# First block tile of a conv-gated MLP on one Trainium2 core: the plain tile's end and the down weights behind the copy of its first chain, down units between its last chains, three squares by transfers

## The chip, the cores and the metric

The kernel runs on one core of one Trainium2 chip. The metric is device time in microseconds (us). The time before is 1180.66 us, the median of three runs (1180.66 to 1180.72). The engines are TensorE (PE, with its weight loads as PEld), VectorE (DVE), ScalarE (ACT), GpSimd (POOL) and SyncE (SP), which issues loads. Each works off its own instructions in order and waits on semaphores for the others.

## The reference: what is computed

The reference is a trunk of two layers over 512 tokens of width 1024, in float32. Each layer has a mixer (an mLSTM or a band attention, with memory cross-attention) and then the part that matters here, a gated MLP with a causal convolution of width 3 and 2816 hidden columns:

```python
def conv_ffn(h, w_up, conv_w, conv_b, w_down):
    u, g = jnp.split(h @ w_up, 2, axis=-1)
    g = causal_dwconv(g, conv_w, conv_b)
    return (jax.nn.silu(g) * u) @ w_down

x = x + conv_ffn(rmsnorm(x, norm_ffn_g[l]), ffn_w_up[l], ffn_conv_w[l], ffn_conv_b[l], ffn_w_down[l])
```

The RMS norm divides each token by the root of the mean square over its 1024 features. The kernel keeps activations transposed: eight tiles `xT[0..7]` of 128 features by 512 tokens, so the mean square is a sum over the eight tiles and over the partitions.

## The kernel before

**Precision.** Each float32 operand is split into a high part (a cast on ACT, line 144) and a low part (a subtraction on DVE, line 145). A product is three matmuls (lines 198 to 200): high by high, high by low, low by high.

**The norm.** `OutProjection.finish` (line 720) ends the mixer of a layer. For each tile j it adds the projection to `xT[j]` on DVE (line 725), stores the tile by a transfer on POOL's queue (line 726, pinned in order), hands it to `norm.add` and scales it into a high and a low part (lines 341 and 342). `Norm.add` squares the tile on ACT. Tile 0's square starts the sum; those of tiles 1 to 4 (`j < SENT`, with `SENT = 5`) are added to it by accumulating transfers on POOL's queue (line 296), each of which waits for the one before; tile 5's square starts a second sum (`new`); tiles 6 and 7 are added to that on DVE (line 298). After tile 7 `norm.join()` (line 301) adds the first sum to the second on DVE. `Norm.finish` splits the sum, adds it over the partitions with matmuls by ones (line 311), and forms the row of inverse roots.

**The MLP.** The 2816 hidden columns are 22 tiles. Tiles 0 and 1 are plain: a gate chain and an up chain of 24 full-width matmuls each (`plain_chain`), then `plain_gate` (line 778): gate by norm row (L780), last tap on ACT (L763), two taps on DVE (L756), SiLU on ACT (L784); then `plain_end` (line 787): the multiplication with the up part on DVE (L788), and `keep`, which splits the result into the high and low part of `hid`.

Tiles 2 to 21 are block tiles: the gate and up products of a tile are computed together by a scheme with seven half-size products instead of eight, on sums and differences of weight blocks and of activations. The activations' sums are made in `block_sums` (lines 797 and 806), the weights' ones in `Forms` (L995). A step (line 915) has seven chains of 12 half-width matmuls: a11, a12, s2, s1, s3, a22, s4. Four of them (a11, s2, s3, a22) use the same PSUM buffer r1, and between two of them ACT copies the result out (line 933 for a11, line 923 for the others). s1 and s4 share r3; DVE reads it (line 946) before s4 may start. DVE adds the a12 chain at line 936. In the same step the next tile's weights are prepared (`nxt`) and the previous tile's taps, SiLU and gating are done (`tail`).

**Down units.** The product with `w_down` is cut into units of a few hidden tiles by 128 output columns. Units of the step are computed into two PSUM buffers (tag `tr`), copied by ACT (line 832) and added in memory by a transfer of POOL's queue (line 836). Tile 2's step has four units (hidden tiles 0 and 1), the steps behind it mostly two. Their weights are loaded on SP's queue (line 157), and split by `split_down` into the buffer pair `wh2`, `wl2`, of which there is one.

**The order.** Inside `later` the order of PE, ACT and DVE is the one written out by hand (`manual_schedule`, line 903). Outside it, in `finish`, `first_plain` and `second_plain`, a planner places instructions by its own cost model. Before the change `plain_end` of tile 1 and `split_down` stand in `second_plain` (lines 893 and 896), so the planner places them; in the step of tile 2 all four units stand behind the last chain, and those of later tiles behind s3.

Of the kernel before, what the change touches and what calls it, by code (L numbers as in the profile page):

```python
# [18 lines left out]
S = 512  # L19
KT = D // P  # L20
# [9 lines left out]
FT = DFF // P  # L30
# [12 lines left out]
PLAIN, LAST, LATE = 2, 6, 8  # L43
# [4 lines left out]
LATE_ROW = {11: 2, 12: 3, 13: 4, 14: 5, 15: 0, 16: 1, 17: 6, 18: 7}  # L48
UNITS = {PLAIN + i: tuple((i, j) for j in range(*LOADS[i][2:])) for i in range(len(LOADS))}

H, SENT = S // 2, 5


def f(ap):
# [4 lines left out]
def trunk(  # L59
# [34 lines left out]
    def sb(tag, shape, dtype=F32):  # L94
        count[0] += 1
        return pool.tile(shape, dtype, tag=tag, name=f"{tag}{count[0]}", bufs=bufs[tag])

    def ps(tag):
        count[0] += 1
        return psum.tile([P, S], F32, tag=tag, name=f"p{tag}{count[0]}", bufs=pbufs[tag])  # L100
# [101 lines left out]
    def project(w, c0, act, tag="mm", parts=None):  # L202


        n = len(act)
        wh, wl = parts or weights(rows(w, c0, P), n, P)
        o = ps(tag)
        for k in range(n):
            mm3(o, wh[:, k, :], wl[:, k, :], act[k][0], act[k][1], k == 0, k == n - 1)
            yield  # L210
        return o

    def run(gen):
        while True:
            try:
                next(gen)
            except StopIteration as end:
                return end.value
# [57 lines left out]
    def logarithms():  # L276

        pin(A.preload_act_table_set("natural_log_exp_and_others"))

    class Norm:  # L280
# [22 lines left out]
        def finish(self):  # L303


            parts = [sb("t", [P, S], F32R) for _ in range(2)]
            split(*parts, self.acc)
            yield 7.4
            o = ps("sc")
            for i, part in enumerate(parts):  # L310
                nc.tensor.matmul(o, onesr, part, start=i == 0, stop=i == 1)
            v, r, t = sb("rb", [P, S]), sb("t", [P, S]), sb("t", [P, S])
            A.activation(t, o, AF.Ln, scale=1.0 / D, bias=eps)
            V.tensor_scalar(v, o, 1.0 / D, EPS, op0=ALU.mult, op1=ALU.add)
            A.activation(r, t, AF.Exp, scale=-0.5)
            A.activation(t, r, AF.Square)
            yield 4
            V.scalar_tensor_tensor(t, t, -0.5, v, op0=ALU.mult, op1=ALU.mult)
            self.row = sb("rb", [P, S])
            V.scalar_tensor_tensor(self.row, t, 1.5, r, op0=ALU.add, op1=ALU.mult)  # L320
# [18 lines left out]
    def scaled(t, g):  # L339
        hi, lo = sb("u", [P, S], F32R), sb("u", [P, S], F32R)  # L340
        A.activation(hi, t, AF.Copy, scale=g)
        V.scalar_tensor_tensor(lo, t, g, f(hi), op0=ALU.mult, op1=ALU.subtract)  # L342
        return hi, lo
# [86 lines left out]
    norm = Norm()  # L430
# [44 lines left out]
    with tc.manual_schedule(engines={mybir.EngineType.PE, mybir.EngineType.Activation, mybir.EngineType.DVE}):  # L475

        logarithms()
        w = ps("mm")
# [17 lines left out]
        def step(products, os_, k, order):  # L496
            for a, b in order:
                for i, o in enumerate(os_):
                    c = slice(i * P, (i + 1) * P)
                    st, mv = kv[k][a], memT[k][b]  # L500
                    first, last = (k, (a, b)) == (0, order[0]), (k, (a, b)) == (KT - 1, order[-1])
                    if products == "keys":
                        nc.tensor.matmul(o, st[:, c], mv, start=first, stop=last)
                    else:
                        nc.tensor.matmul(o, mv[:, c], st[:, MEM:], start=first, stop=last)
# [194 lines left out]
    class OutProjection:  # L700
# [19 lines left out]
        def finish(self, mixer):  # L720
            logarithms()
            norm = mixer.norm
            for j in range(KT):
                o = self.o[j] if j in self.o else run(project(self.w, j * P, self.mixes))
                V.tensor_add(xT[j], xT[j], o)
                pin(G.dma_start(xspill[j], xT[j]))
                norm.add(xT[j], sent=j < SENT, new=j == SENT)
                mixer.act.append(scaled(xT[j], mixer.gain[:, j : j + 1]))
                if j == KT - 1:
                    norm.join()  # L730
                for _ in range(EARLY[mixer.l].get(j, 0)):
                    next(mixer.forms)

    class ChannelMixer:
# [148 lines left out]
        def second_plain(self):  # L883
            og = run(self.plain_chain(1, False, self.next_gate))
            ou = run(self.plain_chain(1, True))
            prep = Forms(self, PLAIN)
            prep.split_up()
            prep.sums()
            prep.split_second()
            acc = self.plain_gate(1, og)  # L890
            prep.sum_third()
            prep.split_sums()
            self.plain_end(acc, ou)
            prep.sum_fourth()
            prep.split_gate()
            prep.split_down()
            return prep

        def later(self, prep):


            tail = None
            with tc.manual_schedule(
                engines={mybir.EngineType.PE, mybir.EngineType.Activation, mybir.EngineType.DVE}
            ):
                for j in range(PLAIN, FT):
                    self.beside()
                    tail, prep = self.step(j, prep, Forms(self, j + 1) if j + 1 < FT else None, tail)
            for part in (
                tail.last_block, tail.scaled, tail.first_tap, tail.scaled_up,  # L910
                tail.second_tap, tail.third_tap, tail.silu, tail.gated, tail.split,
            ):
                part()

        def step(self, j, w, nxt, tail):
            def then(o, *names):
                for name in names if o is not None else ():
                    getattr(o, name)()

            def sum_products(o, r, w, i):  # L920

                self.products(r, w, self.t(i))
                A.copy(o, r[:, :H])  # L923

            new = Tail(self, j)
            late = self.load_late(LATE_ROW[j]) if j in LATE_ROW else None
            then(tail, "last_block", "scaled")
            w.split_fourth()
            then(tail, "scaled_up")
            r1, r2, new.r3 = ps("mm"), ps("mm"), ps("sc")  # L930
            new.up, new.u3, new.pre = sb("t", [P, S]), sb("t", [P, S]), sb("t", [P, S])
            self.products(r1, w.a11, self.b(0, 0), True)
            A.copy(new.up[:, :H], r1[:, :H])  # L933
            then(tail, "first_tap", "second_tap", "third_tap")
            self.products(r2, w.a12, self.b(1, 0), True)
            V.tensor_tensor(out=new.up[:, :H], in0=new.up[:, :H], in1=r2[:, :H], op=ALU.add)
            sum_products(new.up[:, H:], r1, w.s2, 2)
            then(tail, "silu")
            then(nxt, "sums")
            self.products(new.r3, w.s1, self.t(1), True)  # L940
            then(tail, "gated")
            then(nxt, "split_second", "sum_third")
            sum_products(new.u3[:, :H], r1, w.s3, 3)
            then(tail, "split")
            then(nxt, "split_up")
            V.tensor_tensor(out=new.pre[:, H:], in0=new.u3[:, :H], in1=new.r3[:, :H], op=ALU.add)
            if j > PLAIN:
                w.down_products(0, 2)
            then(nxt, "split_sums", "sum_fourth")
            if j > PLAIN:  # L950
                w.add_down(0)
            then(nxt, "split_gate")
            if j > PLAIN:
                w.add_down(1)
                then(nxt, "split_down")
            sum_products(new.pre[:, :H], r1, w.a22, 4)
            if j > PLAIN:
                w.down_products(2, 4)
            self.products(new.r3, w.s4, self.b(1, 1))
            if j == PLAIN:  # L960
                w.down_products(0, 2)
                w.add_down(0)
                w.add_down(1)
                w.down_products(2, 4)
                then(nxt, "split_down")
            w.add_down(2)
            w.add_down(3)
            if late is not None:
                self.late_row(LATE_ROW[j], late)
            return new, nxt  # L970
# [102 lines left out]
    def channel_mixer(mixer):  # L1073
        mixer.first_plain()
        mixer.buffers()
        prep = mixer.second_plain()
        run(mixer.forms)
        mixer.later(prep)
        reload_x()
        return mixer.hid[FT - LAST :]  # L1080

# [295 lines left out]
    mixer = ChannelMixer(0, col["gffn"][:, 0:8], more_rows)  # L1377
# [14 lines left out]
    norm = norm2  # L1392
# [123 lines left out]
    mixer = ChannelMixer(1, col["gffn"][:, 8:16], lambda: None)  # L1516
# [125 lines left out]
```

## Time and profile before

| What | Value |
|---|---|
| Median of three runs | 1180.66 us |
| The profiled execution's own time | 1179.68 us |
| Its span | 1178.0 us |
| PE busy | 1161.6 us |
| DVE busy | 987.0 us |
| ACT busy | 747.1 us |
| Step of tile 2, layer 0 | 296.00 to 314.38 us |
| Step of tile 2, layer 1 | 851.46 to 869.97 us |

How to read it: the profile is one execution, with times in us from the span's start. In a timeline a row has start, duration, engine, line, operation, output and input, the count of merged instructions, and in brackets the idle time before it with what ended it. In the waits a row has the waiting engine and line, what it waited for, and the total, the count and the longest. Matmuls are pipelined, and their ends are modelled, so a PE that is shown as busy may still lose time between two starts.

### The profile page before, as it was taken

The numbers are of one execution on the slowest core, as the hardware profiler recorded it, in microseconds if no ns is written. First come the engines' busy times: TensorE is split into PE (matmuls) and PEld (weight loads), VectorE is DVE, ScalarE is ACT, GpSimd is POOL, SyncE is SP. The second block draws the span as 40 slices with busy tenths as digits, with TensorE's granted clock in tenths as the row PEclk, the third lists the DMA queues.
The fourth block names the chain that finished last, engine by engine and source line by source line (L and its number), as shares of the span: only waits on it lengthen the run. The fifth ranks groups of instructions, "written<-read, shape, count | busy, mean of one in ns | idle before, by whom it ended". The sixth has DMA issues, their size and how long they took to land.

```text
span 1178.0 us, 19355 instructions
## 1 busy us (share of the span) xinstructions
PE 1161.6 (99%) x7221; PEld 1035.6 (88%) x7221; DVE 987.0 (84%) x1766; ACT 747.1 (63%) x1345; POOL 158.2 (13%) x262
## 2 busy tenths in 40 slices
PE   9999999999999999999999999999999999999997
PEld 9988888887899999999888888778789999999986
DVE  6776788889799988888788888897979998888865
ACT  6448677656666655555676576777666765555545
POOL 1111101011121222111020000101010111111100
PEclk9999999999999999999999999999999999999999
DMA  8645315256368877776573323236535667777651
GB/s 294 217 109 148 77 55 152 78 148 184 111 159 189 201 191 193 177 176 133 159 222 94 90 67 100 88 106 177 154 116 152 154 148 177 178 179 171 134 162 72
DMA packets 205904, 173.37 MB, mean 147 GB/s; under 512 B 9352, under 2 KB 178030, under 8 KB 205810
## 3 DMA queue, kind: packets, MB, share of 16 engines
q1 hardware_dynamic: 184914, 123.93, 35.7%
q0 software_dynamic: 20320, 47.15, 20.0%
q8 instruction: 57, 0.93, 0.3%
q10 hardware_dynamic: 576, 1.05, 0.2%
q14 instruction: 37, 0.30, 0.1%
HBM read 133.09 MB, written 40.85 MB: 148 GB/s over the span
## 4 chain that ended last, share of the span: by engine, by line
PE 87%; DVE 4%; issue 4%; ACT 3%; DMA 2%; POOL 0%; POOLq 0%; DVEq 0%; ACTq 0%
PE pmm L198 16%; PE pmm L199 16%; PE pmm L200 16%; PE ptr L199 5%; PE ptr L198 5%; PE ptr L200 5%; PE psc L198 4%; PE psc L200 4%; PE psc L199 4%; PE psc L612 2%; PE ptr L1464 1%; DMA rb<-t 1%; DVE wl L145 1%; PE ptr L1485 1%; PE ptr L1486 1%
## 5 line engine op out<-in xcount | busy, mean ns | idle before, releaser
L198 PE MATMUL pmm<-u,wh 128*128 128x256 f32 (+1 forms) x992 | 334.7, 338 | 0.2 <-ACT u L144 0.2
L199 PE MATMUL pmm<-u,wh 128*128 128x256 f32 (+1 forms) x992 | 331.9, 335 | 0.5 <-DVE u L342 0.5
L200 PE MATMUL pmm<-u,wl 128*128 128x256 f32 (+1 forms) x992 | 332.3, 335 | 0.0
L145 DVE TENSOR_TENSOR wl<-wr,wh 128x1024 fp32r<-128x1024 f32 (+4 forms) x172 | 193.4, 1125 | 77.1 <-ACT wh L144 76.5
L144 ACT CAST wh<-wr 128x1024 fp32r<-128x1024 f32 (+4 forms) x172 | 167.0, 972 | 77.4 <-PE pmm L199 33.7
L200 PEld LDWEIGHTS pmm<-u,wl 128*128 128x128 f32 x992 | 186.3, 188 | 18.8
L199 PEld LDWEIGHTS pmm<-u,wh 128*128 128x128 f32 x992 | 186.6, 188 | 17.2 <-DVE u L342 0.9
L198 PEld LDWEIGHTS pmm<-u,wh 128*128 128x128 f32 x992 | 186.4, 188 | 16.6 <-ACT u L144 1.0
L198 PE MATMUL ptr<-u,wh 128*128 128x512 f32 x272 | 106.5, 392 | 0.0
L199 PE MATMUL ptr<-u,wh 128*128 128x512 f32 x272 | 106.3, 391 | 0.0
L200 PE MATMUL ptr<-u,wl 128*128 128x512 f32 x272 | 105.8, 389 | 0.0
L144 ACT CAST fh<-pt 128x512 fp32r<-128x512 f32 x120 | 74.8, 624 | 38.2 <-DVE pt L995 35.3
L198 PE MATMUL pmm<-u,fh 128*128 128x256 f32 x320 | 89.2, 279 | 3.1 <-ACT t L933 2.1
L923 ACT COPY t<-pmm 128x256 f32<-128x256 f32 x120 | 45.0, 375 | 69.3 <-PE pmm L200 69.2
L199 PE MATMUL pmm<-u,fh 128*128 128x256 f32 x320 | 88.6, 277 | 0.0
L200 PE MATMUL pmm<-u,fl 128*128 128x256 f32 x320 | 88.4, 276 | 0.0
L145 DVE TENSOR_TENSOR fl<-pt,fh 128x512 fp32r<-128x512 f32 x120 | 82.4, 687 | 3.9 <-ACT fh L144 0.7
L756 DVE SCALAR_TENSOR_TENSOR t<-t,cols,t 128x511 f32<-128x511 f32 x88 | 65.9, 749 | 8.1 <-ACT t L763 6.7
L198 PEld LDWEIGHTS pmm<-u,fh 128*128 128x128 f32 x320 | 60.1, 188 | 6.0 <-ACT t L933 2.5
L198 PE MATMUL psc<-u,wh 128*128 128x256 f32 (+1 forms) x208 | 63.2, 304 | 0.0
L200 PE MATMUL psc<-u,wl 128*128 128x256 f32 (+1 forms) x208 | 62.9, 303 | 0.0
L199 PE MATMUL psc<-u,wh 128*128 128x256 f32 (+1 forms) x208 | 62.9, 302 | 0.0
(358 smaller groups left out, 2629.0 us busy)
## 6 DMA issues: line engine op xcount, KB each, us to landing
wr<-in_ffn_w_up_dram SPq DMA_DIRECT2D x48, 512.0 KB, 8.5
pt<-in_ffn_w_up_dram SPq DMA_DIRECT2D x40, 512.0 KB, 7.6
wr<-in_ffn_w_down_dram SPq DMA_DIRECT2D x32, 512.0 KB, 5.2
wr<-in_a_w_in_dram SPq DMA_DIRECT2D x20, 512.0 KB, 3.7
xspill<-bias POOLq DMA_DIRECT2D x32, 256.0 KB, 6.9
without_row<-bias POOLq DMA_DIRECT2D x24, 256.0 KB, 4.3
wr<-in_w_kv_dram SPq DMA_DIRECT2D x12, 512.0 KB, 3.9
without_row<-t POOLq DMA_DIRECT2D x24, 256.0 KB, 4.1
```

Of the source, the lines that this page charges most:

```text
L144: high = A.copy(hi, src) if on_act else V.tensor_copy(hi, src)
L145: low = V.tensor_tensor(out=lo, in0=src, in1=f(hi), op=ALU.subtract)
L198: nc.tensor.matmul(o, lh, rh, start=first, stop=False, skip_group_check=more)
L199: nc.tensor.matmul(o, lh, rl, start=False, stop=False, skip_group_check=more)
L200: nc.tensor.matmul(o, ll, rh, start=False, stop=last, skip_group_check=more)
L612: nc.tensor.matmul(o, a, b, start=first and i == 0, stop=i == 1)
L756: V.scalar_tensor_tensor(acc[:, n:], src[:, : S - n], self.fw[:, c * FT + j : c * FT + j + 1], acc[:, n:], op0=ALU.mult, op1=ALU.add,)
L923: A.copy(o, r[:, :H])
L1464: nc.tensor.transpose(tp[:, b * P : (b + 1) * P], es[T, h][:, b * P : (b + 1) * P], ident)
L1485: nc.tensor.matmul(o2[:, s * P :], w, hi_at(pts[h], s, s, TT - s), start=s == 0, stop=False)
L1486: nc.tensor.matmul(o2[:, s * P :], w, lo_at(pts[h], s, s, TT - s), start=False, stop=s == TT - 1)
```

## The change

Three edits in one:

1. `plain_end` of tile 1 and `split_down` of tile 2 leave `second_plain` and stand in the hand-written step of tile 2, behind ACT's copy of the a11 chain.
2. The four units of tile 2 stand as in the other steps: two behind s3, two behind a22. The next tile's `split_down` stands ahead of the copy of a22.
3. `SENT` is 4 instead of 5: the squares of tiles 1 to 3 are added by transfers, tile 4's starts the second sum, tiles 5 to 7 are added on DVE. `join` stands ahead of tile 7's `norm.add`.

```diff
-H, SENT = S // 2, 5
+H, SENT = S // 2, 4
...
                 pin(G.dma_start(xspill[j], xT[j]))
+                if j == KT - 1:
+                    norm.join()
                 norm.add(xT[j], sent=j < SENT, new=j == SENT)
                 mixer.act.append(scaled(xT[j], mixer.gain[:, j : j + 1]))
-                if j == KT - 1:
-                    norm.join()
...
             prep.split_sums()
-            self.plain_end(acc, ou)
             prep.sum_fourth()
             prep.split_gate()
-            prep.split_down()
-            return prep
+            return prep, (acc, ou)
...
             self.products(r1, w.a11, self.b(0, 0), True)
             A.copy(new.up[:, :H], r1[:, :H])
+            if tail is None:
+                self.plain_end(*plain)
+                w.split_down()
             then(tail, "first_tap", "second_tap", "third_tap")
...
-            if j > PLAIN:
-                w.down_products(0, 2)
+            w.down_products(0, 2)
             then(nxt, "split_sums", "sum_fourth")
-            if j > PLAIN:
-                w.add_down(0)
+            w.add_down(0)
             then(nxt, "split_gate")
-            if j > PLAIN:
-                w.add_down(1)
-                then(nxt, "split_down")
+            w.add_down(1)
+            then(nxt, "split_down")
             sum_products(new.pre[:, :H], r1, w.a22, 4)
-            if j > PLAIN:
-                w.down_products(2, 4)
+            w.down_products(2, 4)
             self.products(new.r3, w.s4, self.b(1, 1))
-            if j == PLAIN:
-                w.down_products(0, 2)
-                w.add_down(0)
-                w.add_down(1)
-                w.down_products(2, 4)
-                then(nxt, "split_down")
             w.add_down(2)
             w.add_down(3)
```

More of the change, by code (lines that the diff above doesn't have):

```diff
@@ L892, in second_plain, with later @@
             prep.split_sums()
-            self.plain_end(acc, ou)
             prep.sum_fourth()
             prep.split_gate()
-            prep.split_down()
-            return prep
-        def later(self, prep):
+            return prep, (acc, ou)
+        def later(self, prep, plain):
             tail = None
@@ L907, in later @@
                     self.beside()
-                    tail, prep = self.step(j, prep, Forms(self, j + 1) if j + 1 < FT else None, tail)
+                    tail, prep = self.step(j, prep, Forms(self, j + 1) if j + 1 < FT else None, tail, plain)
             for part in (
@@ L913, in later, with step @@
                 part()
-        def step(self, j, w, nxt, tail):
+        def step(self, j, w, nxt, tail, plain):
             def then(o, *names):
@@ L1075, in channel_mixer @@
         mixer.buffers()
-        prep = mixer.second_plain()
+        prep, plain = mixer.second_plain()
         run(mixer.forms)
-        mixer.later(prep)
+        mixer.later(prep, plain)
         reload_x()
```

## The prediction

> **What bounds the kernel now.** I read the page first, then the waits of TensorE (PE), the table by stage around the first block tile (tile 2) of each layer, and there the timelines of PE, ScalarE (ACT), VectorE (DVE) and GpSimd (POOL).
>
> ```profile
> PE 1161.6 (99%) x7221; PEld 1035.6 (88%) x7221; DVE 987.0 (84%) x1766; ACT 747.1 (63%) x1345; POOL 158.2 (13%) x262
> ```
> ```profile
> PE pmm L198 <- ACT t L933: 2.1, 2, 1.1
> PE psc L198 <- DVE t L946: 1.7, 2, 0.8
> PE pmm L482 <- DVE mcf L131: 1.1, 1, 1.1
> PE pmm L198 <- ACT t L923: 1.1, 2, 0.6
> PE psc L311 <- ACT t L144: 0.7, 2, 0.4
> PE pmm L199 <- DVE u L342: 0.5, 1, 0.5
> ```
> PE is the bound nearly everywhere. Of its six longest waits five lie at places that this change touches: three inside the step of tile 2 (for the copy of its first chain at L933, the copy at L923, the addition at L946), each once in each layer; two at the norm before it (L311, L342).
>
> ```profile
> 296.00:314.38 18.38, 16.10 (x111) 14.54 (x110) 11.68 (x17) 9.68 (x17) 1.11 (x2) 1.00 0.32 101
> 314.38:326.60 12.22, 12.22 (x98) 11.73 (x97) 11.21 (x18) 9.78 (x19) 3.54 (x7) 1.00 0.39 137
> 833.00:851.46 18.46, 17.87 (x76) 14.22 (x77) 18.38 (x34) 12.55 (x21) 0.00 (x0) 1.00 0.40 115
> 851.46:869.97 18.51, 15.96 (x110) 14.39 (x108) 13.06 (x20) 10.83 (x18) 1.09 (x2) 1.00 0.31 98
> ```
> Each row has a stretch, its length, busy time (and instructions) of PE, weight loads (PEld), DVE, ACT and POOL, the granted clock and the DMA. In this order: the step of tile 2 in layer 0; the step of tile 3 behind it; in layer 1 the stretch ahead of tile 2, and its step. What does a step of tile 2 lose? It has seven chains of 12 half-width matmuls and four down units of 6 full-width ones; an ordinary step has the same chains and two units.
>
> ```profile
> 308.92 0.23 PE ptr L198
> ...
> 314.16 0.23 PE ptr L200
> ```
> These are the first and last of tile 2's 24 unit matmuls in the chain of waits: one per 0.228 us, so a unit takes 1.37, and a chain of half-width ones as much. The ordinary step took 12.22 and PE was busy in all of it, so tile 2 needs 12.22 + 2 x 1.37 = 14.96. It took 18.38 and 18.51: 3.4 and 3.55 us are lost. The listed waits make up 1.0 + 0.55 + 0.85 = 2.4 of that in a layer; the other 1.0 lies in matmul ends, which are modelled, and restarts, some 0.3 for a wait. The clock is 1.00 throughout.
>
> By the PE busy column alone the loss would be 18.38 - 16.10 = 2.3. [...]
>
> **Edit 1: plain tile's end and down weights behind the copy.** ACT in layer 0, then in layer 1:
>
> ```profile
> 296.93 1.15 ACT L784 ACTIVATE t<-t 128x512 f32<-128x512 f32 x2
> 297.99 1.04 ACT L144 CAST wh<-wr 128x1024 fp32r<-128x1024 f32 x1
> 298.93 0.61 ACT L144 CAST u<-t 128x512 fp32r<-128x512 f32 x1
> 299.44 0.36 ACT L933 COPY t<-pmm 128x256 f32<-128x256 f32 x1
> ```
> ```profile
> 852.52 1.28 ACT L784 ACT_TABLE_LOAD   x1
> 853.82 0.63 ACT L784 ACTIVATE t<-t 128x512 f32<-128x512 f32 x1
> 854.36 0.80 ACT L763 ACTIVATE t<-t,cols 128x512 f32<-128x512 f32 x1
> ...
> 857.62 0.63 ACT L784 ACTIVATE t<-t 128x512 f32<-128x512 f32 x1
> ```
> In layer 0 the copy at 299.44 stood behind the cast of the down weights (297.99) and one of a plain tile's end (298.93), though its chain (296.00 + 1.37) was done at about 297.4. With these moved behind it, it starts at about 298.0, and PE's wait of 1.0 for it goes. What is late next? On ACT, behind the copy, stand now the cast of plain tile 1's end (it waits for the multiplication on DVE, and that for the second SiLU), the down weights' cast, and the copy of the s2 chain, for which PE's s3 chain waits. On DVE, the addition of the second chain and the sums for tile 3 stand behind the low parts of both.
>
> So the end S of the second SiLU sets a clock. DVE in layer 0:
>
> ```profile
> 299.06 1.23 DVE L145 TENSOR_TENSOR wl<-wr,wh 128x1024 fp32r<-128x1024 f32 x1 [0.17 <-ACT wh L144]
> 300.20 0.68 DVE L145 TENSOR_TENSOR u<-t,u 128x512 fp32r<-128x512 f32 x1
> 300.80 0.41 DVE L936 TENSOR_TENSOR t<-t,pmm 128x256 f32<-128x256 f32 x1
> ```
> S + 0.7 (a multiplication of the shape at 300.20), + 0.55 (small cast, 298.93 to 299.44, and a hand-over), + 1.05 the weights' cast, + 1.14 its low part (299.06 to 300.20), + 0.4 the addition at L936: the sums for tile 3 (L995) begin at S + 3.85. From there an ordinary step shows how long the first down copy takes, on DVE and on ACT:
>
> ```profile
> 319.25 0.68 DVE L995 TENSOR_TENSOR pt<-pt 128x512 f32<-128x512 f32 x1
> ```
> ```profile
> 323.92 0.58 ACT L832 COPY bias<-ptr 128x512 f32<-128x512 f32 x1
> ```
> 4.67, less some 0.3 for the previous tile's parts, which tile 2's step has not: 4.4. + 0.6 for the copy, which frees the buffer of the third unit; + two units and the s4 chain, 4.1, and a restart. The step ends at S + 13.1, or when PE has done its 14.96, whichever is later.
>
> **Edit 2: units behind the chains s3 and a22.** The first two units come between s3 and a22, the others between a22 and s4. Their 2.74 us each time cover the copy at L923 (wait 0.55) and the addition at L946 (0.85); without that cover both waits stay. Added is a wait: tile 3's down weights use the same buffer, so their cast on ACT waits for the fourth unit, with the copy of a22, two down copies and tile 3's first cast and copy behind it. That is about 2.3 us of ACT work behind the fourth unit, and the s4 chain and two chains of tile 3 (4.1) cover it: nothing; uncovered, at most the 2.3. On SP's queue the load that reuses the down buffer (up weights of tile 4) leaves about 1 us later in layer 0, some 15 us ahead of its use a step further on: nothing.
>
> **Edit 3: three squares by transfers, join ahead of the last square.** POOL and DVE in layer 0, then in layer 1:
>
> ```profile
> 271.65 0.86 POOL L296 DMA_DIRECT2D rb<-t  x1 [4.28 <-ACT u L341]
> ```
> ```profile
> 274.57 0.69 DVE L995 TENSOR_TENSOR pt<-pt,wr 128x512 f32<-128x512 f32 x1 [0.73 <-DMA wr<-in_ffn_w_up_dram]
> 275.18 0.69 DVE L298 TENSOR_TENSOR rb<-rb,t 128x512 f32<-128x512 f32 x1
> 275.78 0.75 DVE L342 SCALAR_TENSOR_TENSOR u<-fl,cols,u 128x512 fp32r<-128x512 f32 x1
> 276.86 0.69 DVE L301 TENSOR_TENSOR rb<-rb,rb 128x512 f32<-128x512 f32 x1 [0.33 <-DMA rb<-t]
> ```
> ```profile
> 823.56 0.85 POOL L296 DMA_DIRECT2D rb<-t  x1 [3.58 <-ACT u L144]
> ...
> 828.70 0.85 POOL L296 DMA_DIRECT2D rb<-t  x1 [3.73 <-ACT wh L144]
> ```
> ```profile
> 827.60 0.69 DVE L725 TENSOR_TENSOR fl<-fl,pmm 128x512 f32<-128x512 f32 x1 [0.84 <-PE pmm L200]
> 829.89 0.69 DVE L995 TENSOR_TENSOR pt<-pt,wr 128x512 f32<-128x512 f32 x1 [1.60 <-DMA wr<-in_ffn_w_up_dram]
> ```
> The fourth transfer, issued at 271.65, landed some 5.1 later and held the join 0.33. It goes, and the spills behind it on POOL's queue leave earlier. In its place DVE gets one addition of 0.60 (275.18 to 275.78). The join needs only the third transfer, landed by 271.65 and 828.70, since the fourth waited for it. So in layer 0 the join fills the 0.73 that DVE stands still: DVE is ahead by 0.73 + 0.33 - 0.60 = 0.5 from there on. In layer 1 the join moves out of a busy stretch (18.38 of 18.46) into the wait of 1.60, and the extra addition into that of 0.84: 0.6 ahead. Bounds: 0 (the planner orders otherwise) to 1.06. PE's waits at L311 and L342, with restarts 0.7 in layer 0 and 1.4 in layer 1, may go too, but count only where PE and not S ends the step.
>
> **The sum.** Layer 0: S was 296.93 + 1.15 = 298.1, with edit 3 297.6; the step ends at 310.7 instead of 314.38, gain 3.7. Bounds: S unmoved 3.2; PE alone (296.00 - 0.7 + 14.96 = 310.3) 4.1.
>
> Layer 1: the second SiLU ended only at 857.62 + 0.63 = 858.25, and at that S the step would end at 871.35, later than 869.97. But S moves: the table load stood behind the cast that goes. Its input is
>
> ```profile
> 850.80 0.74 DVE L756 SCALAR_TENSOR_TENSOR t<-t,cols,t 128x510 f32<-128x510 f32 x1
> ```
> done at 851.54, with edit 3 at 850.95. Then the table load, 1.28, the first SiLU, with L763 0.54 behind its start: L763 from 852.8 to 853.6, two taps of 0.74, second SiLU 855.2 to 855.8. End 868.9, gain 1.1. Bounds: -1.4 (S as before) to 2.6 (L763 ahead of the table load). I take 1.1, since it follows the order in which this layer's rows stand.
>
> Behind both steps PE stays busy, so what is gained stays: 4.8 in all. The profiled execution, 1179.68 (span 1178.0), would become 1174.9; it lies 1.0 below the median of the three runs, 1180.66, which becomes 1175.9.
>
> **Rivals.**
> - *PE alone ends both steps.* The planner puts taps and SiLU early enough. Layer 0 gains 4.1, layer 1 ends at 851.46 - 1.4 + 14.96 = 865.0 and gains 5.0: 9.1, 1171.6. For it: sums and weights ahead of the taps could give way. Against: the 18.38 of 18.46 that DVE works there. Chance 0.08.
> - *Layer 1 gives back a part.* S stays near 858.25 there: 3.2 - 1.4 = 1.8, 1178.9. For it: the second SiLU came 3.8 behind the first in layer 1 (853.82, 857.62), but right behind it in layer 0 (296.93, two in one row). [...] Chance 0.18, half of it within 0.2%.
> - *Slower: the join holds DVE.* If the planner thinks transfers faster than they are, it puts the join ahead of tile 7's addition, DVE stands there until the third transfer lands, and everything behind, S too, is later by d in both layers. The sum is 2d - 1.8: slower than before from d = 0.9; d = 2.5, half of a transfer's 5.1, gives +3.2, 1183.9. Against: the third had landed at 271.65 and 828.70, and DVE stood waiting for a load until 274.57 and 829.89. Chance 0.07.
> - *No change.* The planner leaves the plain end ahead of the copy, or what is saved waits further on, for loads. Against: the copy is ahead of it in the hand-written order, and no other wait of PE in the list is over 0.5. 1180.7, chance 0.06.
>
> **How the numbers follow.** The forecast has 0.61: 1175.9, its own range 1174.0 (4.1 + 2.6) to 1177.9 (3.2 - 0.4; -0.4 is layer 1 without edit 3's 0.6 and with a copy and a cast of 0.9 ahead of L763). The second rival takes the range to 1179.0, a part of the first to 1173.3. A measurement of this kernel tells about 0.2% (2.4 us) from no change: faster 0.61 + 0.08 + 0.09 = 0.78; same 0.09 + 0.06 = 0.15; slower 0.07.
>
> **What would show it.** Right: no L946 in the waits of PE, L933 and L923 shrunk; the L933 copy ahead of the plain end's cast; a step of tile 2 of 15 to 15.7 us in layer 0 and 16 to 18 in layer 1, where PE waits for the L923 copy of s2 or for a down copy (L832); six transfers at L296. Wrong: a layer-1 step of over 18.5, a join that waits over 1 us with tile 7's addition behind it, or shorter steps with the saved time lost further on.

## The result and the profile after

The changed kernel takes 1178.45 us (median; 1176.45 to 1182.96), the kernel before beside it 1180.77 (1179.96 to 1182.57): ratio 0.9981, 95% interval 0.9974 to 0.9988, that is 2.3 us less where 4.8 were forecast. The profiled execution took 1180.58 us (span 1178.4) at a mean granted clock of 0.996; it lies 2.1 above its median, for which a cause is given below.

The table of stretches of the changed kernel, columns as before. In each layer first from the first tile's addition (L725) to the step of tile 2, then the step:

```profile
253.53:297.49 43.96, 43.03 (x189) 35.06 (x187) 41.98 (x68) 34.65 (x52) 8.13 (x13) 1.00 0.58 164
297.49:313.02 15.53, 15.30 (x109) 14.12 (x108) 11.75 (x17) 8.47 (x16) 1.11 (x2) 1.00 0.38 116
806.91:855.24 48.33, 44.82 (x182) 35.91 (x181) 41.41 (x67) 32.98 (x51) 7.00 (x11) 0.93 0.55 158
855.24:870.82 15.58, 15.32 (x109) 14.12 (x108) 13.16 (x19) 9.93 (x19) 1.08 (x2) 1.00 0.28 84
```

The same stretches of the kernel before (its step's end taken at the next step's first matmul, 314.22):

```profile
252.75:296.00 43.25, 42.87 (x189) 34.95 (x188) 41.00 (x66) 32.40 (x50) 8.99 (x14) 1.00 0.65 184
808.56:851.48 42.92, 41.88 (x183) 33.75 (x182) 40.26 (x65) 31.53 (x50) 7.85 (x12) 1.00 0.68 184
```

The steps fell from 18.2 and 18.5 to 15.5 and 15.6. But the stretch ahead of them grew, by 0.7 in layer 0 and by 5.4 in layer 1, where also the granted clock is 0.93. What lies between (layer 0's step to layer 1's first addition) took 493.9 to 494.4 us in every kernel of this study, and what lies behind (layer 1's step to the last matmul) 300.5, so these four stretches hold what the edits do. They don't hold the whole difference between two profiled executions: layer 0's first addition began at 252.75 us in the kernel before and at 253.05 to 254.25 in the others. In the three traces compared with it (changed kernel, moves alone, early join with five squares) nearly all of this difference is there after the first 8 to 12 us, ahead of everything that was edited.

The waits of PE:

```profile
PE psc L311 <- ACT t L144: 1.8, 1, 1.8
PE pmm L199 <- DVE u L342: 1.5, 2, 0.9
...
PE pmm L198 <- ACT u L341: 1.1, 1, 1.1
```

The three waits inside the step (before: L933, L923, L946) are gone. Those at the norm grew: L311 from 0.7 to 1.8 in all, L342 from 0.5 to 1.5, and 1.1 for L341 is new. In layer 1 it is 1.8 + 1.1, and 0.6 of the wait for L342. VectorE in layer 1 there, changed kernel:

```profile
822.55 0.68 DVE L298 TENSOR_TENSOR rb<-rb,t 128x512 f32<-128x512 f32 x1
823.15 0.68 DVE L145 TENSOR_TENSOR u<-t,u 128x512 fp32r<-128x512 f32 x1
827.39 0.69 DVE L301 TENSOR_TENSOR rb<-rb,rb 128x512 f32<-128x512 f32 x1 [3.56 <-DMA rb<-t]
828.00 0.75 DVE L342 SCALAR_TENSOR_TENSOR u<-fl,cols,u 128x512 fp32r<-128x512 f32 x1
828.66 1.22 DVE L145 TENSOR_TENSOR wl<-wr,wh 128x1024 fp32r<-128x1024 f32 x1
829.80 0.68 DVE L725 TENSOR_TENSOR fl<-fl,pmm 128x512 f32<-128x512 f32 x1
```

The planner put the join (L301) ahead of tile 6's low part (L342), of a low part of weights and of tile 7's addition (L725). VectorE stood there for 3.56 us, until the third transfer landed, 6.3 behind its issue on POOL's queue:

```profile
821.00 0.86 POOL L296 DMA_DIRECT2D rb<-t  x1 [3.00 <-issue]
```

All three came late, and with them tile 7's scaling and square on ACT. PE's starts behind it:

```profile
830.29 0.39 PE L200 MATMUL pmm<-u,wl 128*128 128x512 f32 x1
831.81 0.50 PE L198 MATMUL pmm<-u,wh 128*128 128x512 f32 x1 [1.13 <-ACT u L341]
832.93 0.50 PE L199 MATMUL pmm<-u,wh 128*128 128x512 f32 x1 [0.62 <-DVE u L342]
...
833.97 0.40 PE L200 MATMUL pmm<-u,wl 128*128 128x512 f32 x1
836.12 0.80 PE L311 MATMUL psc<-t,onesr 128*128 128x512 f32 x1 [1.75 <-ACT t L144]
...
837.14 0.63 PE L199 MATMUL psc<-u,wh 128*128 128x512 f32 x1
837.56 0.63 PE L200 MATMUL psc<-u,wl 128*128 128x512 f32 x1
...
842.53 0.40 PE L199 MATMUL psc<-u,wh 128*128 128x512 f32 x1
842.77 0.40 PE L200 MATMUL psc<-u,wl 128*128 128x512 f32 x1
```

Read the distance of starts, not the durations. It is 0.24 at 842.5 and 0.42 between 837.1 and 837.6. The granted clock of that stretch is the last column but two:

```profile
836.71:842.26 5.55, 5.55 (x15) 4.29 (x14) 4.56 (x9) 4.56 (x8) 0.00 (x0) 0.50 0.35 98
```

For 5.55 us the clock was halved, and 13 starts, each 0.2 late, cost 2.6 us. The idle time ahead of it, distance less 0.23, is 1.3 + 0.9 + 1.9 = 4.1. The runs agree with this as far as they go: those of the changed kernel at a mean clock of 0.999 took 1176.45, 1177.24 and 1177.52, those at 0.995 and 0.996 1178.84 to 1182.96, and 0.003 of 1178 us is 3.5 us. So the profiled execution seems to hold a cost that a part of the others have not; only this one has a trace.

ACT in the steps, layer 0 and then layer 1:

```profile
299.06 0.37 ACT L931 COPY t<-pmm 128x256 f32<-128x256 f32 x1 [1.73 <-PE pmm L200]
299.33 0.64 ACT L784 ACTIVATE t<-t 128x512 f32<-128x512 f32 x1
300.72 0.62 ACT L144 CAST u<-t 128x512 fp32r<-128x512 f32 x1 [0.76 <-DVE t L788]
301.24 1.04 ACT L144 CAST wh<-wr 128x1024 fp32r<-128x1024 f32 x1
302.19 0.36 ACT L921 COPY t<-pmm 128x256 f32<-128x256 f32 x1
```
```profile
856.81 0.37 ACT L931 COPY t<-pmm 128x256 f32<-128x256 f32 x1 [0.61 <-PE pmm L200]
857.08 0.64 ACT L784 ACTIVATE t<-t 128x512 f32<-128x512 f32 x1
```

The copy (L931, before L933) waits for PE alone; the planner put the second SiLU behind it. S, that SiLU's end, is 299.97 and 857.72, and the steps end at 313.02 and 870.82: S + 13.05 and S + 13.10, the 13.1 of the prediction. In layer 1 the step is short since it began late: S itself came 50.8 behind the layer's first addition (806.91), in the kernel before 49.7 (808.56 to 858.25). In layer 0 too S came 1.1 later: 46.4 behind the first addition (253.53), before 45.3 (252.75 to 298.08).

### The profile page after: what moved, and what is told of

Same layout as the page of the kernel before. It is cut to its first block, busy times and chain, and to the rows that moved or that the text cites. A ratio compares the mean times of both kernels' runs of the same rounds, so it can differ in the third digit from the quotient of the medians.

```text
span 1178.4 us, 19340 instructions
## 1 busy us (share of the span) xinstructions
PE 1164.1 (99%) x7221; PEld 1038.0 (88%) x7221; DVE 987.8 (84%) x1768; ACT 746.8 (63%) x1345; POOL 156.7 (13%) x260
## 3 DMA queue, kind: packets, MB, share of 16 engines
q10 hardware_dynamic: 576, 1.05, 0.2%
## 5 line engine op out<-in xcount | busy, mean ns | idle before, releaser
L144 ACT CAST wh<-wr 128x1024 fp32r<-128x1024 f32 (+4 forms) x172 | 166.9, 972 | 80.1 <-PE pmm L199 31.6
L199 PEld LDWEIGHTS pmm<-u,wh 128*128 128x128 f32 x992 | 186.5, 188 | 18.2 <-DVE u L342 2.1
L144 ACT CAST fh<-pt 128x512 fp32r<-128x512 f32 x120 | 74.9, 625 | 41.4 <-DVE pt L986 38.7
L921 ACT COPY t<-pmm 128x256 f32<-128x256 f32 x120 | 45.1, 375 | 68.6 <-PE pmm L200 68.5
L200 PE MATMUL psc<-u,wl 128*128 128x256 f32 (+1 forms) x208 | 63.9, 307 | 0.0
```

Source lines behind the costliest of these rows:

```text
L144: high = A.copy(hi, src) if on_act else V.tensor_copy(hi, src)
L199: nc.tensor.matmul(o, lh, rl, start=False, stop=False, skip_group_check=more)
L200: nc.tensor.matmul(o, ll, rh, start=False, stop=last, skip_group_check=more)
```

## The experiments

**The theory** from these rows: the two moves in the step gain what was forecast for them, and edit 3 takes a part back, because VectorE meets the join before the transfer has landed (3.56 us before, in layer 1), and everything behind it in VectorE's order shifts. **The rivals:** the number of squares and not the join's place costs the time (it moves the planner's order, and work from POOL's queue to VectorE); or the moves gain less than the steps show, since layer 1's step only began late.

Each kernel was timed beside the kernel before, and its ratio is to those runs; medians of different rows are not to be subtracted. The last two columns hold the stretches defined above, from each kernel's profiled execution.

| Kernel | Median us | Ratio, 95% interval | Layer 0: ahead, step | Layer 1: ahead, step |
|---|---|---|---|---|
| before | 1180.77 | | 43.25, 18.22 | 42.92, 18.49 |
| changed | 1178.45 | 0.9981 (0.9974 to 0.9988) | 43.96, 15.53 | 48.33, 15.58 |
| moves alone | 1177.61 | 0.9968 (0.9956 to 0.9979) | 43.46, 15.25 | 43.33, 18.09 |
| edit 3 alone | 1182.39 | 1.0009 (1.0000 to 1.0017) | 44.14, 16.93 | 46.41, 17.81 |
| join at its old place | 1179.34 | 0.9983 (0.9974 to 0.9992) | 47.0, 15.6 | 41.36, 17.67 |
| early join, five squares | 1187.05 | 1.0051 (1.0037 to 1.0065) | 49.62, 15.03 | 47.58, 17.04 |
| early join, three squares | 1175.46 | 0.9951 (0.9938 to 0.9963) | 42.47, 16.05 | 41.80, 17.70 |
| squares by layer | 1175.05 | 0.9947 (0.9935 to 0.9960) | 43.79, 15.28 | 41.39, 17.64 |
| edit 1 alone | 1183.42 | 1.0019 (1.0011 to 1.0028) | 43.23, 17.88 | 42.99, 21.18 |
| edit 2 alone | 1177.90 | 0.9974 (0.9964 to 0.9984) | 42.95, 16.47 | 43.41, 17.44 |
| weights first | 1178.74 | 0.9977 (0.9968 to 0.9986) | 43.23, 16.61 | 43.12, 17.52 |
| end behind the second copy | 1179.14 | 0.9981 (0.9972 to 0.9990) | 43.33, 16.63 | 42.85, 17.56 |
| weights behind the sums | 1174.60 | 0.9948 (0.9934 to 0.9961) | 42.46, 15.91 | 41.63, 17.44 |
| end moved in layer 0 only | 1174.58 | 0.9941 (0.9927 to 0.9954) | 43.13, 15.28 | 41.38, 16.50 |

**The two moves alone** (changed kernel with edit 3 undone):

```diff
-H, SENT = S // 2, 4
+H, SENT = S // 2, 5
...
-                if j == KT - 1:
-                    norm.join()
                 norm.add(xT[j], sent=j < SENT, new=j == SENT)
                 mixer.act.append(scaled(xT[j], mixer.gain[:, j : j + 1]))
+                if j == KT - 1:
+                    norm.join()
```

> Edits 1 and 2 alone (five squares, join where it was). Theory A (the two steps gained 2.85 and 2.9 us, and the early join lost it again by holding DVE): the norm stretch is as before, steps of tile 2 of 15.5 us in both layers, 1180.7 - 5.8 = 1174.9 (1174.2 to 1175.6). Rival B (the early join is harmless, the changed kernel's lower clock is chance): about 1178.4, like the changed kernel. Rival C (the moved plain end itself upsets the norm stretch): a wait of over 1 us at L311 or L342 here too, 1177 to 1179.

It gains 3.7 us (1181.28 in the kernel before beside it), more than the whole change, though the two intervals overlap. By the stretches layer 0 gives all of it, 2.8 in both together; in layer 1 the step is 0.4 shorter, but the two stretches together are 61.4 as before. So of theory A's steps of 15.5 only layer 0's came. In layer 1 S sets the end:

```profile
854.95 0.64 ACT L784 ACTIVATE t<-t 128x512 f32<-128x512 f32 x1 [0.89 <-DVE t L756]
856.35 0.62 ACT L144 CAST u<-t 128x512 fp32r<-128x512 f32 x1 [0.76 <-DVE t L788]
856.87 1.04 ACT L144 CAST wh<-wr 128x1024 fp32r<-128x1024 f32 x1
857.82 0.37 ACT L921 COPY t<-pmm 128x256 f32<-128x256 f32 x1
```

S is 855.59, the step ends at 868.64, S + 13.05. The s2 chain's copy (L921, before L923) stands behind the plain end's cast and the weights', and PE waits 1.6 for it.

**Edit 3 alone** (kernel before with four squares and the early join):

```diff
-H, SENT = S // 2, 5
+H, SENT = S // 2, 4
...
+                if j == KT - 1:
+                    norm.join()
                 norm.add(xT[j], sent=j < SENT, new=j == SENT)
                 mixer.act.append(scaled(xT[j], mixer.gain[:, j : j + 1]))
-                if j == KT - 1:
-                    norm.join()
```

> Edit 3 alone (three squares by transfers, join ahead of tile 7's square; steps of tile 2 as before, 18.4). Theory A: DVE waits some 3.5 us at the join in layer 1 with tile 6's low part and tile 7's addition behind it, PE waits some 3.5 us at L341, L342 and L311 and its clock falls for some us; 3 to 6 us slower than before, 1183.7 to 1186.7. Rival B: 1180.7 within 1. My forecast's own reading (DVE 0.5 ahead): 1179.5 to 1180.7.

Alone it costs 1.1 us (interval 0 to 2.0), less than theory A's 3 to 6. The join in layer 1 waits 2.50 us instead of 3.56, and the two stretches of that layer together are 2.8 longer, 1.6 of it by starts of PE that come every 0.40 to 0.43 us instead of 0.23 (838.50 to 841.88); layer 0's are 0.4 shorter.

**The join at its old place** (changed kernel, still four squares): the second hunk just shown, undone.

> The changed kernel with the join back behind tile 7's square and scaling, three squares by transfers kept. Theory A (the place of the join costs, not the number of squares): no wait at the join over 0.5 us, 1174.0 to 1175.5. Rival C2 (the fourth addition on DVE and the order that it brings about cost as much as the join): 1177 to 1179 with waits at L341 or L342 of over 1 us in layer 1.

Layer 1's two stretches fall from 63.9 to 59.0, 2.4 less than before the change: the cost there was the join's place. Theory A's time, 1174.0 to 1175.5, did not come: the whole gains nothing over the changed kernel, since layer 0 now takes 62.6 in its two stretches (changed kernel 59.5, kernel before 61.5). ACT there:

```profile
276.85 1.05 ACT L144 CAST wh<-wr 128x1024 fp32r<-128x1024 f32 x1 [3.47 <-DMA wr<-in_ffn_w_up_dram]
277.80 0.63 ACT L294 ACTIVATE t<-fl 128x512 f32<-128x512 f32 x1
278.34 0.71 ACT L341 ACTIVATE u<-fl,cols 128x512 fp32r<-128x512 f32 x1
```

With four squares the planner puts a cast of weights, whose load lands late, ahead of tile 7's square (L294) and scaling (L341); before, they stood ahead of it. The changed kernel has this too, at 276.46 with 3.33 of wait, and yet its layer 0 is only 0.8 above the moves alone (58.7). It lacks what follows here. With the late join the cast of the norm's sum (L144, t<-rb) starts at 282.15 on ACT instead of 279.58, behind two sums (L797) and one more cast of weights. PE waits a third time, 1.05 for those weights, and from 283.07 to 286.06 its matmuls of 128x512 start every 0.43 us instead of 0.23. So the number of squares does cost in layer 0, through ACT's order: little with the early join, about 3.5 us with the late one.

**The early join with five squares:** the changed kernel with `SENT = 5`.

> The changed kernel with five squares (four transfers) again and the join left ahead of tile 7's addition to the norm: the suspected wait is doubled. Theory A (the early join holds VectorE until the last transfer lands, and all behind it comes later): the join now needs a transfer that is issued 5 to 6 us later, so its row in layer 1 shows a wait of 6 us or more instead of 3.56, one of over 2 us appears in layer 0, and the time is 4 to 9 us above that of the two moves in the step alone (ratio to the kernel before 1.000 to 1.005). Rival B (the loss comes from the number of squares, which moves other work of ScalarE and VectorE, and not from the join's place): with five squares the time is within 1.2 us of the two moves alone (ratio 0.996 to 0.998).

```profile
277.58 0.69 DVE L301 TENSOR_TENSOR rb<-rb,rb 128x512 f32<-128x512 f32 x1 [4.78 <-DMA rb<-t]
...
835.67 0.69 DVE L301 TENSOR_TENSOR rb<-rb,rb 128x512 f32<-128x512 f32 x1 [6.03 <-DMA rb<-t]
```

Waits of 4.78 and 6.03, and 6.0 us slower than before by the ratio, 9.8 above the moves alone, a little more than expected: the theory. From the moves alone this kernel differs in nothing but the join's place, so here the number of squares has no part in it. Both layers have a stretch behind the waits in which PE's starts come every 0.43 us instead of 0.23 (283.79 to 287.63, 841.24 to 844.20), 1.8 and 1.4 us of the cost.

**The early join with three squares:** the changed kernel with `SENT = 3`.

> The changed kernel with three squares (two transfers) and the join left ahead of tile 7's addition: the suspected wait is taken away, since the last transfer is issued one tile earlier, and VectorE gets one addition of 0.6 us more in each layer. Theory A: the join in layer 1 waits under 0.7 us instead of 3.56, the slow stretch of PE behind it is gone, and the time falls by 1 to 2.5 us from the changed kernel's (ratio to the kernel before 0.996 to 0.9975). Rival B (the added additions on VectorE, not the wait, cost the time): another addition makes it 0.5 us or more slower than the changed kernel (ratio over 0.9985).

```profile
273.78 0.69 DVE L301 TENSOR_TENSOR rb<-rb,rb 128x512 f32<-128x512 f32 x1
...
823.89 0.69 DVE L301 TENSOR_TENSOR rb<-rb,rb 128x512 f32<-128x512 f32 x1
```

No wait in either layer, and 5.8 us less than before by the ratio. The join stands as early as in the changed kernel and VectorE has one addition more in each layer, so neither costs: the wait for the transfer does. Taken away or enlarged, it moves the time in its direction. The rival of the additions falls.

**Squares by layer:** the moves alone, with five squares in layer 0 and four in layer 1, the join at its old place.

```diff
-H, SENT = S // 2, 5
+H, SENT = S // 2, (5, 4)
...
-                norm.add(xT[j], sent=j < SENT, new=j == SENT)
+                norm.add(xT[j], sent=j < SENT[mixer.l], new=j == SENT[mixer.l])
```

> The two moves in the step, the join at its old place, five squares in layer 0 and four in layer 1: each layer gets the form that did best there so far. If the gains of the layers are separate and stay (theory A): 2.8 us in layer 0 and 2.4 in layer 1, 5.2 in all, ratio 0.9956 (0.9945 to 0.9967). Rival C (a gain in layer 1 is lost again, by the clock or by loads): no better than the two moves alone, ratio 0.9968 or more.

The gains add up: 6.3 us by the ratio, 2.4 in each layer's two stretches. Only layer 0's `SENT` sets it apart from the join at its old place: 3.6e-3 of the time, 4.2 us, is what four squares cost there with the late join, by ACT's order and the half-rate starts behind it together (3.5 by the two stretches).

**Edit 1 alone and edit 2 alone** (of the moves alone, one half each; the other half as in the kernel before).

> Edit 1 alone: the plain tile's end and the down weights behind the copy of the first chain; the units stay at the end of the step, five squares, the join at its old place. If the two moves of the step each take their own waits (as the prediction had it): PE's wait for the first copy goes, those for the s2 or s3 copy and the addition behind a22 stay, and the step of layer 0 falls from 18.4 to about 17 us; ratio 0.998 to 0.9995. If the end of the second SiLU sets everything behind it and the units are needed as its cover: the step of layer 0 stays within 0.5 us of 18.4 and the ratio is 0.9995 or more.

> Edit 2 alone: the units behind the chains s3 and a22; the plain tile's end and the down weights stay ahead of the step, five squares, the join at its old place. If the two moves take their own waits: PE's waits for the copy of s3 and for the addition behind a22 go, that for the first copy stays, and the steps fall by 1.2 to 2 us each, ratio 0.997 to 0.9985. If one move does nothing without the other: the steps stay within 0.5 us, ratio 0.9995 or more.

PE's waits in layer 1, with edit 1 alone and then with edit 2 alone:

```profile
859.74 0.39 PE L198 MATMUL pmm<-u,wh 128*128 128x256 f32 x1 [1.62 <-ACT t L921]
863.30 0.52 PE L198 MATMUL pmm<-u,fh 128*128 128x256 f32 x1 [1.87 <-ACT t L921]
```
```profile
854.93 0.38 PE L198 MATMUL pmm<-u,fh 128*128 128x256 f32 x1 [1.10 <-ACT t L933]
860.96 0.50 PE L199 MATMUL ptr<-u,wh 128*128 128x512 f32 x1 [0.75 <-DVE u L145]
```

The moves don't act alike. Edit 2 gains 3.1 us by itself; the waits for the copy of s3 and for the addition behind a22 are covered. Edit 1 by itself costs 2.2: PE's wait for the first copy goes, but the copies behind it (s2, s3, a22) now stand behind the second SiLU, with no units between to cover it. A part of the 2.2 is the rate of the starts: in the profiled execution matmuls of 128x256 start every 0.21 us instead of 0.11 from 863.84 to 866.85, behind the two waits of layer 1 just shown, and lose 1.4 us there. On top of edit 2 it brings 1.2 in layer 0's step and costs 0.65 in layer 1's, where the SiLU comes later; with the stretches ahead counted 0.7 and 0.6, and the ratios (0.9968 with both, 0.9974 with edit 2 alone) don't tell the two kernels apart. So nearly all of what the moves gain is edit 2's. Of the two expectations for edit 1 the prediction's own fell, and that of the SiLU held.

**Weights first** (the moves alone, with `w.split_down()` ahead of `self.plain_end(*plain)`):

> Edits 1 and 2 alone, with the down weights' split ahead of the plain end behind the copy. Theory A with the clock S + 13.1 (S the end of the second SiLU): the weights' cast (1.05) and low part (1.14) leave the chain behind S, PE alone ends the step: 15.0 to 15.1 us a step, 0.5 less than with e1 in each layer, 1173.9. Rival (the chain of steps behind S is held by something else, DVE's sums or the copies): 15.5 as in e1, 1174.9.

```profile
299.88 1.23 DVE L145 TENSOR_TENSOR wl<-wr,wh 128x1024 fp32r<-128x1024 f32 x1 [1.04 <-ACT wh L144]
301.02 0.68 DVE L145 TENSOR_TENSOR u<-t,u 128x512 fp32r<-128x512 f32 x1
301.62 0.68 DVE L788 TENSOR_TENSOR t<-psc,t 128x512 f32<-128x512 f32 x1
```

A miss: 16.6 and 17.5 us. In layer 0 S is 298.63, but the multiplication (L788) starts at 301.62, since VectorE meets the weights' low part first and waits 1.04 for its cast. The work swapped on ACT came back on VectorE.

**The end behind the second copy** (the moves alone, `plain_end` moved on behind the copy of the s2 chain, `split_down` left):

> The two moves in the step alone, but the plain tile's end still later: the down weights' cast stays behind the first copy, and the end, which waits for the second SiLU, comes behind the copy of the s2 chain. Theory A (in layer 1 the step was held since that copy stood behind the plain end's cast, and so behind the SiLU): PE's waits for the copy of s2 go, and the step in layer 1 falls from 18.1 to 15.0 to 16.2 us, layer 0 stays at 15.0 to 15.8; ratio 0.9945 to 0.996. Rival D (the SiLU holds the step by VectorE's order as well: sums and low parts stand behind it): the wait moves on to the down copy, the layer 1 step is 17 us or more, ratio 0.9965 to 0.998.

The wait for the s2 copy goes, as hoped; in its place PE waits 0.9 in each layer for a down copy (L832), since the multiplication and its low part now delay the sums for tile 3. Rival D: the SiLU holds the step through VectorE as well.

**Weights behind the sums** (the early join with three squares, `split_down` behind tile 3's first sums):

```diff
             if tail is None:
                 self.plain_end(*plain)
-                w.split_down()
...
             then(nxt, "sums")
+            if tail is None:
+                w.split_down()
```

> The changed kernel with three squares (two transfers), and the down weights' split moved on behind the next tile's first sums, so that in the chain behind the second SiLU stand neither the cast (1.05 on ScalarE) nor its low part (1.14 on VectorE). If the end S of the second SiLU sets the step through that chain (S + 13.1 in nearly every run so far): the step ends at about S + 12 in both layers, the copy of s2 comes 0.9 earlier, the step falls to 15 to 15.3 us in layer 0 and 16.4 to 17 in layer 1, and the time lies 1.5 to 2.5 us under that of three squares alone (ratio 0.993 to 0.994). Rival: the split only moves, and the first unit or the s3 chain waits for the weights' low part instead: S + 13 stays, ratio 0.9945 to 0.9955.

```profile
853.75 0.39 PE L198 MATMUL pmm<-u,wh 128*128 128x256 f32 x1 [0.57 <-ACT t L921]
857.00 0.50 PE L200 MATMUL ptr<-u,wl 128*128 128x512 f32 x1 [1.10 <-DVE wl L145]
```

The copy of s2 came 0.9 earlier behind S (852.05), but the first unit then waited 1.10 for the weights' low part. The steps end at S + 12.9 and S + 12.8, not S + 12: the rival was right, and the ratio is the same as with three squares alone within the intervals.

**The end moved in layer 0 only** (squares by layer, `plain_end` and `split_down` in `second_plain` in layer 1):

> The kernel with the squares by layer (five, then four, the join at its old place) and the units moved in both layers, but the plain tile's end and the down weights behind the first copy in layer 0 only; in layer 1 they stay ahead of the step. If edit 1 costs in layer 1 what the runs of the single edits say (its step 18.09 us with both edits, 17.44 with the units alone): layer 1's step falls from 17.6 to 16.9 to 17.2 and the ratio is 0.994 to 0.9945. Rival: with VectorE freed by the squares the second SiLU comes early enough for edit 1 to cost nothing, and putting the end ahead brings back PE's wait of 1.1 for the first copy: step 17.6 or more, ratio 0.9947 to 0.996.

```profile
296.70:311.98 15.28, 15.28 (x109) 14.11 (x108) 12.41 (x18) 10.49 (x19) 1.11 (x2) 1.00 0.30 87
806.24:847.62 41.38, 41.38 (x183) 33.81 (x182) 40.67 (x65) 31.55 (x50) 6.98 (x11) 1.00 0.61 174
847.62:864.12 16.50, 15.33 (x110) 14.15 (x108) 13.86 (x21) 11.30 (x20) 1.08 (x2) 1.00 0.40 118
```

Layer 1's step fell to 16.50, more than expected, with the wait of 1.2 for the first copy as its only one. PE is busy all through layer 0's step and all through layer 1's stretch ahead of its own. This is the best kernel of the study: 0.9941, 7.0 us below the kernel before; by the intervals it is not told apart from squares by layer (0.9947) and the two kernels with three squares (0.9948 and 0.9951).

## Why the prediction was right or wrong, point by point

**Edits 1 and 2, right in sum.** Without edit 3 the prediction's terms are 3.2 in layer 0 (its bound with S unmoved) and 1.1 - 0.6 = 0.5 in layer 1. The moves alone measured 3.7 in all (by the interval 2.5 to 5.2). By the two stretches of a layer, which is what the terms count, it is 2.8 and 0.0, so layer 1's 0.5 isn't shown, and that the sum hits 3.7 exactly is luck. The rule that the step ends at S + 13.1 held in every kernel with the units between the chains and the end and the weights, in this order, between the first copy and the sums: S + 13.05 to S + 13.2, once 13.4 (five squares with the early join, layer 0). It is put to the test where PE waits in the step; in layer 0's steps of 15.25 to 15.28 PE alone would have ended at the same time. PE alone takes 15.0 to 15.3 (layer 0's steps of 15.03 and 15.28, the latter busy throughout); the count of matmuls had given 14.96, and an estimate from the weight loads (14.54 in the step before the change, at the ordinary step's 11.73 in 12.22) gives 15.15. The order of the planner in layer 1 was as assumed: table load, first SiLU, L763, taps, second SiLU.

**What each of the two brings, half wrong.** Edit 1 was priced at PE's wait of 1.0 for the first copy, with the s2 copy named as what is late next. That is about its worth on top of edit 2 in layer 0 (1.2 by the step, 0.7 with the stretch ahead), but in layer 1 what is late next costs about 0.6 more than the wait removed, and by itself the edit loses 2.2 in all. Both this and the second rival count on ACT and VectorE keeping to the order in which their work is written, and the traces show them doing so. In the changed kernel's layer 0 tile 7's addition ended at 275.52, but ACT stood 3.33 us for a load until 276.46, and tile 7's square, behind that cast, started at 277.41. In the kernel with the weights first VectorE stood 1.04 us for the weights' cast, and the multiplication behind it, whose SiLU had ended at 298.63, started at 301.62.

**Edit 3, wrong: the failing step.** The prediction put it as "the join fills the 0.73 that DVE stands still" and "in layer 1 the join moves ... into the wait of 1.60", 0.6 ahead. It knew well enough when the transfer lands: "landed by 271.65 and 828.70", in layer 1 20.1 behind the layer's first addition, and it landed at 827.32, 20.4 behind it. It was wrong about where the join would stand. The join waits for nothing that tile 7's addition makes, so the planner was free to put it ahead of that, presumably where its cost model had the transfer done (no run shows the model's own times), and VectorE was free for it at 823.83, 3.56 early. In layer 0, where VectorE reached it at 273.57, no wait arose, but the 0.5 that S was to gain there didn't come either: S is 1.1 later than before, with the cast of weights ahead of tile 7's square. The forecast +1.1 for edit 3 became about -1.5 (0.9981 against 0.9968, with overlapping intervals; edit 3 alone gives -1.1): with that 3.7 becomes the measured 2.3.

**The second rival has the number, not the mechanism.** Its 1178.9 lies 0.45 from the measured 1178.45. It has S stay near its old place although the moves are made. But without edit 3 S came 48.4 behind layer 1's first addition (807.22 to 855.59), 1.3 earlier than before; the early join is what made it late. That the number is near is luck.

**The third rival named the mechanism.** Its d was 3.56 in layer 1 (it took 2.5 for its example) and 0 in layer 0, and its price lacked the halved clock (0.50 for 5.55 us, 2.6 us in the profiled execution). It did not make the kernel slower, because the moves' gain was larger than what it took back.

**Not foreseen at all:** that with four squares a cast of weights gets ahead of tile 7's square on ACT in layer 0, and that PE's waits at the norm would be followed by starts at half the clock, 2.6 us in the profiled execution.

**The signs to look for.** Gone or shrunk L933, L923 and L946, the copy ahead of the cast, layer 0's step of 15.5 and six transfers at L296 were as forecast. Layer 1's step of 15.6 lay below the forecast 16 to 18, which looked like success: it was the late start, and the moves alone show 18.1. The sign "a join that waits over 1 us" was among those of wrong, and it is what the timeline shows.

## What to carry to other kernels

An instruction that waits for a transfer is priced by where it will stand in its engine's order, not by where that engine happens to be idle (here it held VectorE for 3.56 us); if a planner may move it, pin it behind the work that must not wait, or take so few transfers that the last has landed. A step that got shorter proves nothing until the stretch ahead of it is measured as well: here layer 1's step fell by 2.9 us, and with the stretch ahead of it the layer got 2.5 longer in the profiled execution. Where several edits go together, price each alone and on top of the others: of the two moves one gains 3.1 by itself, the other loses 2.2, and together they gain hardly more than the first.

## What the runs showed of the hardware

After idle time of PE that came in pieces, matmuls of 128x512 started every 0.43 us instead of 0.23, for 3 to 6 us (with edit 1 alone it was those of 128x256, every 0.21 instead of 0.11); in the changed kernel the granted clock of that stretch was 0.50. This was seen behind gaps of 1.3 + 0.9 + 1.9 within 6 us (changed kernel, layer 1), of 0.4 + 1.2 + 1.2 (join at its old place, layer 0), of 0.9 + 2.3 (edit 3 alone, layer 1), of 1.8 + 2.0 (edit 1 alone, layer 1) and, with the early join and five squares, of 1.4 + 1.3 + 2.1 and 1.9 + 1.3 + 1.5; not behind single gaps of 1.7 (three squares) or 1.8 (join at its old place, layer 1), nor behind 1.6 + 1.1 (edit 1 alone, layer 0). That the idle time is the cause was not tried by itself; it is argued from these places. The largest single gap among them is 2.3 us.

The accumulating transfer of a 128x512 tile landed 6.3 us behind its issue (821.00 to 827.32), where the prediction took 5.1. The six of the changed kernel landed 3.4 to 6.3 us behind, the median at 5.7.
